# Seven zero matmuls ahead of the first projection, two staging tiles moved, and the last row block added up in PSUM

## The chip, the core and the metric

One core of a Trainium2 chip runs the whole program. The metric is the device time of one execution in microseconds (us): the kernel before takes 1064.06 us as the median of three runs (1063.52 to 1064.2). The core has five engines with a queue of instructions each: PE (matrix products; PEld is its loading of weights), DVE (vector), ACT (activations), POOL (general, slower) and SP, which here only issues transfers (DMA). A tile lies in SBUF or, for the sums that PE makes, in one of eight PSUM banks.

## The reference

A transformer block over 1024 tokens with 1024 features. Two groups of eight heads read one combined input projection; group A attends over a window of 128 tokens (two key/value heads, a sink per head), group B over nine chunks of 64 with a learned bias by distance.

```python
n = rms_norm(h, norm1_g[layer])
proj = jnp.einsum('bsd,dp->bsp', n, w_in[layer])
qa, ka, va, qb, kb, vb = jnp.split(proj, split_at, axis=-1)
ya = mixer_a(...); yb = mixer_b(...)
y = jnp.concatenate([rms_norm(ya, out_norm_a_g[layer]), rms_norm(yb, out_norm_b_g[layer])], axis=-1)
h = h + jnp.einsum('bsm,md->bsd', y, w_out[layer])
n2 = rms_norm(h, norm2_g[layer])
u = jnp.square(jax.nn.relu(jnp.einsum('bsd,df->bsf', n2, w_ff1[layer])))
h = h + jnp.einsum('bsf,fd->bsd', u, w_ff2[layer])
return rms_norm(h, final_norm_g)
```

All of it is float32. The kernel takes each product as three products of a high and a low part (high by high, high by low, low by high), summed in PSUM.

## The kernel before

**Start (L216 to L380).** The transposed input x comes in eight slices k of 128 features and two halves t of 512 tokens. `load_xT` (L225) loads a slice, ACT makes its high part (tile `nT`, L233), DVE the low part (L234). The weights of the first three projections, k, q and v of group A (`kA`, `qA0`, `vA`), are loaded and split the same way, those of kA and qA0 in four pieces between the slices. PE then runs, in an order that is written out and pinned from L342 on (`pe_order`): kA and qA0 by turns, two slices at a time, for t = 0 (48 matmuls of 128x512), vA for t = 0 (24), then kA, qA0 and vA for t = 1. After the third slice of kA, t = 1, four transposes turn the row scales `r` into a row `R` (`scales_along`).

`first_place` (L362) scales a projection by `R` into a staging tile `ts_...`, splits it into high and low (ACT L273, DVE or POOL L152) and sends it by 4 (q) or 8 (k) transfers into the tiles `QA` and `KA` that the scores read (L279, L282). For t = 0 the staging tile is one of the buffers that held x (`xs`); for t = 1 of k and q it is one of two buffers called `tst`, which `place` (L264) takes. The next projection, qA1, stages in `tst` too.

**Attention.** A planner interleaves units of attention with the remaining projections. A unit of group A makes scores (`S_A`), takes maxima on DVE (L438) and exponentials on ACT (L439), and normalises the probabilities `P_A`: DVE those of its first block, POOL those of its second (`POOL_NORM`, L545). PE transposes them (`pt_A`), ACT and DVE split the result (`T_A`, L446 and L152), PE multiplies by V (`av_A`). POOL's queue at that place holds, in this order: two scalings of a bias tile `b_A` (L470), the low parts of the weights of qA2 in four pieces (`w_qA`, L152), the two normalisations of the first unit, the low part of the staged qA1.

**SP's queue.** Transfers are issued in one order. Each of them reuses one of eight semaphores and so waits until the transfer eight places ahead has landed.

**Tail (L1198 to L1311).** The MLP's second product ends with the four row blocks 4 to 7 of the lower left quarter. `last_product` (L1276) adds 12 matmuls per block onto the bank that already holds the sum before; blocks 4, 6 and 5 are whole (512 columns), and DVE adds the bank to the residual `C` (tile `h`). For the last block, 7, DVE adds what the bank holds ahead of time (L1268), and the last product goes into two fresh banks `end0` and `end1` of 256 columns. `final` (L1198) is a generator per block: ACT squares and sums the rows, DVE and ACT make the reciprocal root `rf` of their mean, the rows are multiplied by it and the gain, and two transfers write the block out. In it, the halves (`fo`) of blocks 4, 5 and 6 are made by one DVE operation with the gains in PSUM (L1237) and by POOL and ACT (L1217, L1241). For block 7 DVE adds `end0` and `end1` to `C`, ACT squares `C`, POOL multiplies `C` by the gain (L1227), and at last DVE (640 columns) and ACT (384) multiply by `rf`. ACT issues the last transfer, SP the others (L1244).

## Time and profile before

| what | value |
|---|---|
| three runs, median (range) | 1064.06 us (1063.52 to 1064.2) |
| the profiled execution | 1064.61 us, of it 1062.5 us from its first to its last instruction (the span) |
| PE busy | 1048.2 us of the span |
| DVE, ACT, POOL busy | 702.4, 584.3, 421.1 us |
| first matmul, from the span's start | 5.04 us |

Times inside the span count from its start. A row of the timeline has start, duration, engine, line, operation, out<-in, shape and a count where like instructions are merged; square brackets tell how long the engine was idle before and what released it. PEclk is the share of TensorE's clock that was granted. The duration of a matmul goes from issue to its end, and matmuls overlap, so the pace of PE is read from the starts of groups.

### The profile page before, as it was taken

The numbers are of one execution on the slowest core, as the hardware profiler recorded it, in microseconds if no ns is written. First come the engines' busy times: TensorE is split into PE (matmuls) and PEld (weight loads), VectorE is DVE, ScalarE is ACT, GpSimd is POOL, SyncE is SP. The second block draws the span as 40 slices with busy tenths as digits, with TensorE's granted clock in tenths as the row PEclk, the third lists the DMA queues.
The fourth block names the chain that finished last, engine by engine and source line by source line (L and its number), as shares of the span: only waits on it lengthen the run. The fifth ranks groups of instructions, "written<-read, shape, count | busy, mean of one in ns | idle before, by whom it ended". The sixth has DMA issues, their size and how long they took to land.

```text
span 1062.5 us, 14416 instructions
## 1 busy us (share of the span) xinstructions
PE 1048.2 (99%) x5052; PEld 874.1 (82%) x5052; DVE 702.4 (66%) x1120; ACT 584.3 (55%) x1012; POOL 421.1 (40%) x326
## 2 busy tenths in 40 slices
PE   8999999999999999999999999999999999999997
PEld 6888888888888888888888888888888888888886
DVE  5577775767676765696534324436879877778667
ACT  7677786666574565675544554455533333333346
POOL 1476796334350243305564454345015024024026
PEclk9999999999999999999999999999999999999999
DMA  9954536253584442215544535416997535532004
GB/s 329 261 147 136 144 108 162 89 130 112 131 282 170 140 159 100 104 56 177 183 136 159 181 116 178 160 64 247 367 401 267 179 121 165 180 116 91 1 1 159
DMA packets 90440, 170.17 MB, mean 160 GB/s; under 512 B 7808, under 2 KB 43648, under 8 KB 90368
## 3 DMA queue, kind: packets, MB, share of 16 engines
q1 hardware_dynamic: 90080, 169.06, 48.1%
q8 instruction: 40, 0.66, 0.3%
q14 instruction: 32, 0.26, 0.1%
q10 hardware_dynamic: 288, 0.20, 0.1%
HBM read 105.26 MB, written 45.09 MB: 142 GB/s over the span
## 4 chain that ended last, share of the span: by engine, by line
PE 93%; DVE 3%; DMA 2%; ACT 1%; issue 1%; SPq 0%; DVEq 0%; ACTq 0%
PE f L146 27%; PE f_a L146 16%; PE f_c L146 8%; PE ip_qA L146 4%; PE op_B L146 4%; PE f_b L146 4%; PE ip_vB L146 4%; PE ip_qB L146 4%; PE op_A L146 4%; PE ip_kB L146 3%; PE av_B L146 3%; PE pt_B L149 2%; PE S_B L146 2%; PE S_A L146 1%; PE ip_kA L146 1%; PE av_A L146 1%
## 5 line engine op out<-in xcount | busy, mean ns | idle before, releaser
L146 PE MATMUL f<-X,W 128*128 128x512 f32 x1344 | 306.0, 389 | 0.1
L146 PEld LDWEIGHTS f<-X,W 128*128 128x128 f32 x1344 | 252.0, 188 | 52.9 <-DVE X L152 0.5
L146 PE MATMUL f_a<-V,U 128*128 128x512 f32 x756 | 173.6, 389 | 0.2 <-DVE bsf L137 0.2
L152 POOL TENSOR_TENSOR U<-u,U 128x1024 fp32r<-128x1024 f32 x32 | 80.4, 2512 | 226.9 <-PE f_c L146 134.9
L146 PEld LDWEIGHTS f_a<-V,U 128*128 128x128 f32 x756 | 141.9, 188 | 30.1 <-DVE bsf L137 0.6
L152 POOL TENSOR_TENSOR W<-T,W 128x1024 fp32r<-128x1024 f32 x29 | 75.6, 2609 | 141.6 <-ACT W L981 141.6
L146 PE MATMUL f_c<-V,U 128*128 128x512 f32 x384 | 88.4, 389 | 0.0
L146 PEld LDWEIGHTS f_c<-V,U 128*128 128x128 f32 x384 | 72.1, 188 | 15.0
L981 ACT ACTIVATE V<-Z 128x1024 fp32r<-128x1024 f32 x32 | 33.9, 1060 | 89.7 <-PE f_a L146 44.6
L1030 DVE TENSOR_TENSOR k<-f,k 128x1024 f32<-128x1024 f32 x24 | 29.3, 1221 | 60.7 <-PE f L146 60.7
L981 ACT ACTIVATE V<-w 128x1024 fp32r<-128x1024 f32 x24 | 25.4, 1060 | 78.9 <-issue 34.2
L152 POOL TENSOR_TENSOR W<-w,W 128x1024 fp32r<-128x1024 f32 x23 | 56.3, 2449 | 30.9 <-ACT W L981 30.8
L152 DVE TENSOR_TENSOR V<-w,V 128x1024 fp32r<-128x1024 f32 x24 | 47.6, 1985 | 27.1 <-ACT V L981 27.1
L981 ACT ACTIVATE U<-u 128x1024 fp32r<-128x1024 f32 x56 | 58.5, 1044 | 11.5 <-DMA ud<-k 7.1
L439 ACT ACTIVATE P_B<-P_B,nm_B 128x640 f32<-128x640 f32 (+2 forms) x64 | 44.3, 693 | 23.9 <-DVE nm_B L438 12.9
L1024 ACT ACTIVATE k<-f 128x1024 f32<-128x1024 f32 x24 | 24.6, 1026 | 59.1 <-PE f L146 59.1
L152 DVE TENSOR_TENSOR T_B<-pt_B,T_B 128x512 fp32r<-128x512 f32 (+2 forms) x72 | 39.7, 552 | 21.6 <-ACT T_B L446 21.3
L981 ACT ACTIVATE W<-T 128x1024 fp32r<-128x1024 f32 x32 | 33.9, 1058 | 35.5 <-PE f L146 21.1
L146 PE MATMUL ip_vB<-nT,w_vB 128*128 128x512 f32 x192 | 52.0, 399 | 0.9 <-DVE T_B L152 0.9
L146 PE MATMUL op_A<-w_o,y 128*128 128x512 f32 x192 | 52.2, 397 | 0.7 <-DVE h L773 0.4
L146 PE MATMUL ip_qB<-nT,w_qB 128*128 128x512 f32 x192 | 51.5, 396 | 0.0
L146 PE MATMUL ip_kB<-nT,w_kB 128*128 128x512 f32 x192 | 51.3, 396 | 0.0
(233 smaller groups left out, 2056.9 us busy)
## 6 DMA issues: line engine op xcount, KB each, us to landing
w<-in_w_ff_dram SPq DMA_DIRECT2D x64, 512.0 KB, 4.7
u<-ud SPq DMA_DIRECT2D x56, 512.0 KB, 4.7
ud<-k SPq DMA_DIRECT2D x48, 512.0 KB, 3.2
KkB<-ts_kB SPq DMA_DIRECT2D x64, 128.0 KB, 2.3
yd<-y SPq DMA_DIRECT2D x14, 512.0 KB, 2.8
y<-yd SPq DMA_DIRECT2D x14, 512.0 KB, 6.3
xs<-in_xT_dram SPq DMA_DIRECT2D x16, 256.0 KB, 5.3
xr<-in_x_dram SPq DMA_DIRECT2D x8, 512.0 KB, 7.0
```

Of the source, the lines that this page charges most:

```text
L146: pe(nc.tensor.matmul(*args, **kw))
L149: pe(nc.tensor.transpose(*args))
L152: engine.tensor_tensor(lo, full, f(hi), ALU.subtract)
L439: nc.scalar.activation(pr[:, :n], pr[:, :n], AF.Exp, bias=nm, scale=-1.0, accum_out=sm)
L981: nc.scalar.activation(w[0], full, AF.Copy)
L1024: nc.scalar.activation(kept[p], ps, AF.Copy)
L1030: dve.tensor_tensor(v, ps, v, ALU.add)
```

## The change

Three edits. First, a tile `busy` of 128x512 zeros is set by DVE, and PE multiplies it seven times into a PSUM tile that nobody reads, ahead of everything else; the tile takes one of the four buffers of `xr`, so that tile's pool is laid out in another order too. Second, `first_place` stages t = 1 of kA and qA0 in pages (a pool of 35 equal tiles) and no longer in `tst`. Third, for block 7 ACT copies the residual into the two banks `end0` and `end1`, the matmuls add onto it, and ACT squares and DVE multiplies by the gain straight from the banks; block 5's first half moves from DVE to two POOL operations.

```diff
@@ constants
+EARLY = 7
@@ start
     sps = sp_.enter_context(tc.tile_pool(name="sps", bufs=1, space=PSUM))
+    pe_order["on"] = True
+
+    busy = sp.tile([P, HALF], F32R, tag="xr", bufs=4, name="busy")
+    nc.vector.memset(f(busy), 0.0)
+    idle_ps = sps.tile([P, HALF], F32, tag="r", bufs=2, name="idle_ps")
+    for n in range(EARLY):
+        matmul(idle_ps, busy[:, :P], busy, start=n == 0, stop=n == EARLY - 1)
...
-    pe_order["on"] = True
     wk, k_steps = proj_weight(KA0, "kA", dve, 4)
...
-        st = sp.tile([P, 2, HALF], F32R, tag="xs", bufs=6, name=f"ts_{name}_{t}") if kind != "v" and t == 0 else None
+        st = None
+        if kind != "v":
+            st = page([P, 2, HALF], f"ts_{name}_{t}") if t else sp.tile([P, 2, HALF], F32R, tag="xs", bufs=6, name=f"ts_{name}_{t}")
@@ final
             ss, to = square(tmp[:, cs[0]], h[0], "last", base)
             base_of(ss, to, base)
+            if tb == 5:
+                pool.tensor_tensor(tmp[:, cs[0]], h[0], gfb[:, cs[0]], ALU.mult)
         else:
             for m in range(2):
                 c = slice(m * 2 * P, (m + 1) * 2 * P)
-                dve.tensor_tensor(h[0][:, c], ends[m], h[0][:, c], ALU.add)
-                ss, to = square(tmp[:, c], h[0][:, c], "last" if m else "0", base)
-                pool.tensor_tensor(tmp[:, c], h[0][:, c], gfb[:, c], ALU.mult)
+                ss, to = square(h[0][:, c], ends[m], "last" if m else "0", base)
+                dve.tensor_tensor(tmp[:, c], ends[m], gfb[:, c], ALU.mult)
...
-        if tb < 7:
+        if tb == 5:
+            pool.tensor_tensor(tmp[:, cs[0]], tmp[:, cs[0]], r.to_broadcast([P, HALF]), ALU.mult)
+        elif tb < 7:
             dve.scalar_tensor_tensor(tmp[:, cs[0]], h[0], r, gains[0][:, cs[0]], ALU.mult, ALU.mult)
@@ end
-    ends = [fps.tile([P, 2 * P], F32, tag=f"{'ab'[1 ^ g % 2]}1", bufs=1, name="end0")]
+    ends, rest = [], h
+
+    def end_bank(tag):
+
+        m = len(ends)
+        ends.append(fps.tile([P, 2 * P], F32, tag=tag, bufs=1, name=f"end{m}"))
+        in_order[1].activation(ends[m], rest[:, 2 * m * P : 2 * (m + 1) * P], AF.Copy)
+
+    end_bank(f"{'ab'[1 ^ g % 2]}1")
...
-                mm3(ps, ..., alone and n == n0 and i == 0, n > n0 and i == 1, True)
+                mm3(ps, ..., False, n > n0 and i == 1, True)
...
         before = finals[q]
         next(before)
-    last_product(ends[0], 3, slice(0, 2 * P), True)
+        if q == 2:
+            end_bank(f"{'ab'[g % 2]}1")
+    last_product(ends[0], 3, slice(0, 2 * P))
...
-    ends.append(fps.tile([P, 2 * P], F32, tag=f"{'ab'[g % 2]}0", bufs=1, name="end1"))
-    last_product(ends[1], 3, slice(2 * P, HALF), True)
+    last_product(ends[1], 3, slice(2 * P, HALF))
```

The changed kernel's lines are 1 to 21 higher than those before. On PE and DVE, at the very start, the order before is this, PE first (`nT_155` is a high part, `nT_159` a low part):

```order
L146 MATMUL ip_kA_324<-nT_155,w_kA 128x512
L146 MATMUL ip_kA_324<-nT_159,w_kA 128x512
L94 MEMSET ones 128x1
L96 MEMSET eps_76 128x1
L234 SCALAR_TENSOR_TENSOR nT_159<-xs_185,g1c,nT_155 128x512
```

And this with the change:

```order
L147 MATMUL idle_ps<-busy 128x512 x7
L147 MATMUL ip_kA_334<-nT_165,w_kA 128x512
L147 MATMUL ip_kA_334<-nT_169,w_kA 128x512
L95 MEMSET ones 128x1
L97 MEMSET eps_76 128x1
L223 MEMSET busy 128x512
L242 SCALAR_TENSOR_TENSOR nT_169<-xs_195,g1c,nT_165 128x512
```

Nothing else moves on these engines before the tail: one memset and seven matmuls are put in front.

On DVE, where qA1 is staged for the first time (`ts_qA_0`), the order with its waits is this before; the eight DMAHW are the semaphores of transfers:

```order
L438 ISA P_A_2_0_637,nm_A_2_633<-S_A_2_0_636,b_A_318,nsink 128x256 [waits PE_49]
L438 ISA nm_A_2_633 128x1
L152 TENSOR_TENSOR VA_176<-vt_vA_626,VA_176 128x8x64 [waits Activation_49]
L270 SCALAR_TENSOR_TENSOR ts_qA_0_654<-ip_qA_0_588,R_154 128x512 [waits DMAHW4_49,DMAHW3_49,DMAHW5_49,DMAHW2_49,DMAHW6_49,DMAHW1_49,DMAHW7_49,DMAHW0_49,PE_49]
L438 ISA P_A_2_1_667,nm_A_2_633<-S_A_2_1_666,b_A_318,nsink 128x256 [waits PE_49]
```

And this with the change:

```order
L447 ISA P_A_2_0_647,nm_A_2_643<-S_A_2_0_646,b_A_328,nsink 128x256 [waits PE_49]
L447 ISA nm_A_2_643 128x1
L153 TENSOR_TENSOR VA_186<-vt_vA_636,VA_186 128x8x64 [waits Activation_49]
L278 SCALAR_TENSOR_TENSOR ts_qA_0_664<-ip_qA_0_598,R_164 128x512 [waits PE_49]
L447 ISA P_A_2_1_677,nm_A_2_643<-S_A_2_1_676,b_A_328,nsink 128x256 [waits PE_49]
```

The order is the same; the wait for the transfers out of the staging tile is gone.

On DVE at the end of the program the order before is this (`fo_9430` is block 5, `fo_9450` block 7; `qf` and the second `wf` lead to the reciprocal root `rf`):

```order
L137 TENSOR_TENSOR C_7498<-end_9460,C_7498 128x256
L137 RECIPROCAL qf_9433<-uf_9431 128x1
L137 RECIPROCAL rf_9434<-wf_9432 128x1
L137 TENSOR_SCALAR bsf_0_9541<-ssf_0_9539,bsf_1_9457 128x1
L137 TENSOR_TENSOR C_7498<-end_9547,C_7498 128x256
L137 SCALAR_TENSOR_TENSOR fo_9430<-C_7496,rf_9434,gains 128x512
L137 TENSOR_SCALAR wf_9452<-ssf_last,bsf_0_9541 128x1
L137 RECIPROCAL qf_9453<-uf_9451 128x1
L137 RECIPROCAL rf_9454<-wf_9452 128x1
L137 TENSOR_SCALAR fo_9450<-fo_9450,rf_9454 128x640
```

And this with the change, with its waits (block 5 is `fo_9440` and its root `rf_9444`, block 7 `fo_9460`):

```order
L138 TENSOR_TENSOR fo_9460<-end_9470,gfb 128x256 [waits Activation_49]
L138 RECIPROCAL qf_9443<-uf_9441 128x1
L138 RECIPROCAL rf_9444<-wf_9442 128x1 [waits DVE_49]
L138 TENSOR_SCALAR bsf_0_9554<-ssf_0_9552,bsf_1_9467 128x1
L138 TENSOR_TENSOR fo_9460<-end_9513,gfb 128x256 [waits Activation_49]
L138 TENSOR_SCALAR wf_9462<-ssf_last,bsf_0_9554 128x1 [waits DVE_49]
L138 RECIPROCAL qf_9463<-uf_9461 128x1 [waits Activation_49]
L138 RECIPROCAL rf_9464<-wf_9462 128x1 [waits DVE_49]
L138 TENSOR_SCALAR fo_9460<-fo_9460,rf_9464 128x640 [waits DVE_49,Pool_49]
```

The two additions have become two products that wait for ACT's squares, and block 5's product has left DVE. POOL gains the two rows for it in place of its two products of 256 columns:

```order
L1226 TENSOR_TENSOR fo_9430<-C_7352,gfb 128x512
L1226 TENSOR_TENSOR fo_9440<-C_7352,gfb 128x512
L1226 TENSOR_TENSOR fo_9450<-C_7354,gfb 128x512
L1226 TENSOR_TENSOR fo_9460<-C_7354,gfb 128x512
L1232 TENSOR_TENSOR fo_9440<-C_7506,gfb 128x512
L1247 TENSOR_TENSOR fo_9440<-fo_9440,rf_9444 128x512
```

The last of these waits for DVE's `rf_9444`, and SP issues block 5's transfer from it ahead of block 7's.

More of the change, by code (lines that the diff above doesn't have):

```diff
@@ L1280, in last_product @@
             for i in range(2):
-                mm3(ps, (uh[:, i, c], ul[:, i, c]), (wh[:, i, cols], wl[:, i, cols]), alone and n == n0 and i == 0, n > n0 and i == 1, True)
+                mm3(ps, (uh[:, i, c], ul[:, i, c]), (wh[:, i, cols], wl[:, i, cols]), False, n > n0 and i == 1, True)
     for q in (0, 2, 1):
-        last_product(banks["a"][q // 2][:, q % 2], q, slice(0, HALF), False)
+        last_product(banks["a"][q // 2][:, q % 2], q, slice(0, HALF))
         h = acc[1, 0, q // 2][:, q % 2]
```

2 lines of the change are left out of this document (1 added, 1 removed).

## The prediction

> **What bounds the kernel now.** I read the page first, then the waits of PE, then the timeline of the first 60 us and of the last 10, since the change touches only those.
>
> ```profile
> PE 1048.2 (99%) x5052; PEld 874.1 (82%) x5052; DVE 702.4 (66%) x1120; ACT 584.3 (55%) x1012; POOL 421.1 (40%) x326
> PE 93%; DVE 3%; DMA 2%; ACT 1%; issue 1%; SPq 0%; DVEq 0%; ACTq 0%
> PE ip_kA L146 <- ACT w_kA L193: 5.0, 1, 5.0
> ```
>
> PE sets the time: 93% of the chain that ended last, and its one long wait is the 5.0 us before the first matmul. So the change can win only where PE is slow, waits, or has ended. It is slow at the start:
>
> ```profile
> 8.00:10.00 2.00, 2.00 (x6) 1.53 (x5) 1.83 (x4) 1.26 (x3) 0.00 (x0) 1.00 1.01 351
> L146 PE MATMUL ip_qA<-nT,w_qA x5: 628/628/628, 8.3 to 10.0; 128*128 128x512 f32 x5
> L146 PE MATMUL ip_qA<-nT,w_qA x16: 389/389/389, 13.1 to 19.3; 128*128 128x512 f32 x16
> 5.04 3.46 PE L146 MATMUL ip_kA<-nT,w_kA 128*128 128x512 f32 x6 [5.04 <-ACT w_kA L193]
> 8.31 2.76 PE L146 MATMUL ip_qA<-nT,w_qA 128*128 128x512 f32 x6
> 10.87 1.97 PE L146 MATMUL ip_kA<-nT,w_kA 128*128 128x512 f32 x6
> 12.67 1.53 PE L146 MATMUL ip_qA<-nT,w_qA 128*128 128x512 f32 x6
> 19.48 5.60 PE L146 MATMUL ip_vA<-nT,w_vA 128*128 128x512 f32 x24
> 24.92 2.20 PE L146 MATMUL ip_kA<-nT,w_kA 128*128 128x512 f32 x9
> 1056.00:1059.60 3.60, 0.24 (x3) 0.04 (x1) 2.60 (x9) 2.03 (x5) 1.45 (x2) 1.00 0.44 164
> 1059.70:1062.50 2.80, 0.00 (x0) 0.00 (x0) 0.00 (x0) 0.00 (x0) 0.00 (x0) 0.50 0.53 195
> ```
>
> The same matmul takes 628 ns up to 10 us and 389 ns from 13 us on. Six of them start in 10.87-8.31 = 2.56 us, 0.427 us each; later 24 start in 24.92-19.48 = 5.44 us, 0.227 each. The switch lies between 10.87 and 12.67, some 6.5 us after the first matmul. The clock column says 1.00 in the slow stretch too, so it is no witness there; but after PE's last work at 1056.24 it falls from 1.00 to 0.50 by 1059.7. PE's clock is halved when PE rests, and PE begins so. Trainium skill, "TensorE: Matmul & The Clock Gate", section "Part 1: The HAM clock gate (the "warmup" mystery)", has the same two paces, 426.7 and 215.7 ns, and the trace agrees on the first.
>
> **The zero matmuls.** What they cost, and what an earlier full clock is worth:
>
> ```profile
> 0.84 0.06 DVE L96 MEMSET eps<- 128x1 f32 x1
> 4.72 0.75 DVE L234 SCALAR_TENSOR_TENSOR nT<-xs,g1c,nT 128x512 fp32r<-128x512 f32 x1 [3.83 <-ACT nT L233]
> 7.29 0.50 PEld L146 LDWEIGHTS ip_kA<-nT,w_kA 128*128 128x128 f32 x2 [0.50 <-DVE nT L234]
> 13.95 0.75 DVE L234 SCALAR_TENSOR_TENSOR nT<-xs,g1c,nT 128x512 fp32r<-128x512 f32 x1
> 25.09 0.17 DVE L169 RECIPROCAL r<-w_n 128x4 f32<-128x4 f32 x1
> 26.96 0.60 PE L149 MATMUL r<-ident,r 128*128 128x128 f32 x4
> 30.83 5.60 PE L146 MATMUL ip_qA<-nT,w_qA 128*128 128x512 f32 x24
> ```
>
> No row has DVE's memset of 128x512. It follows the memset at 0.84 and lies between that row's 0.06 us and the 0.75 of DVE's 128x512 operation, so it ends between 1.0 and 1.65. Seven matmuls at 0.427 are 2.99 us: they end between 4.0 and 4.7, before the 5.04 at which the data is there, and DVE has nothing else before 4.72. They cost nothing; a start 0.4 later would begin to.
>
> If the clock is full by 7.29, the first projections run so: up to 7.29 PE waits for low parts of nT, as it does now, and from there 44 of the 48 k and q matmuls remain, 44 x 0.227 = 9.97, so vA starts at 17.26 and not at 19.48, 2.2 us earlier. The last low part is ready at 13.95+0.75 = 14.70 and PE wants it at 15.45; the others have more room. vA ends at 22.70. Then the first cut: the four transposes of r cannot start before 25.09+0.17, some 25.3, and from them to qA0, t = 1, it is 30.83-26.96 = 3.87 us. So qA0 starts at 29.2, and 1.65 of the 2.2 us is left.
>
> The second cut is where I expect most of the gain to go:
>
> ```profile
> SPq L282 <- DMA st_qA<-in_w_in_dram: 1.2, 1, 1.2
> 35.45 1.10 SPq L282 DMA_DIRECT2D KA<-ts_kA  x2
> 40.52 1.63 SPq L469 DMA_DIRECT2D b_A<-in_dist_dram  x2
> 45.69 1.77 POOL L470 TENSOR_SCALAR b_A<-b_A 128x256 f32<-128x256 f32 x2 [4.48 <-DMA b_A<-in_dist_dram]
> 47.52 2.82 POOL L152 TENSOR_TENSOR w_qA<-st_qA,w_qA 128x256 fp32r<-128x256 f32 x4
> 50.33 1.83 POOL L545 TENSOR_SCALAR P_A<-P_A,rc_A 128x256 f32<-128x256 f32 x2
> 53.01 0.37 PEld L149 LDWEIGHTS pt_A<-ident,P_A 128*128 128x128 f32 x2
> 51.81 0.69 DVE L270 SCALAR_TENSOR_TENSOR ts_qA<-ip_qA,R 128x512 f32<-128x512 f32 x1 [0.67 <-DMA QA<-ts_qA]
> 52.58 0.63 ACT L273 ACTIVATE ts_qA<-ts_qA 128x512 fp32r<-128x512 f32 x1 [1.13 <-DMA QA<-ts_qA]
> 55.24 0.84 ACT L446 ACTIVATE T_A<-pt_A 128x256 fp32r<-128x256 f32 x2
> ```
>
> The first two transposes of attention (pt_A) read probabilities that POOL normalises until 50.33+1.83 = 52.16. POOL gets to them by a chain that PE has no part in: it idles 4.48 us for the load of b_A, then scales it, splits four weight pieces, and normalises, with no gap from 45.69 to 52.16. And b_A lands when SP's order lets it: SP waits until 35.45 for the landing of st_qA, a load queued behind the input loads, and issues without a long pause from there to 40.52. None of this moves when PE is earlier. PE's second load for pt_A starts some 0.2 after 53.01; it can start at about 52.2. So PE keeps 1.0 us at most and stands still for the rest.
>
> **The staging pages.** They take away DVE's wait of 0.67 us and ACT's of 1.13 for the tiles to be sent. In the trace before PE loses nothing by these. They matter once PE is early: ACT reaches T_A at 55.24 only because its queue is late by them, and the matmul behind T_A would hold PE at today's time. Without them T_A comes some 0.7 us earlier, which is about the lead PE has. I take 0.9 us for the start as a whole; bounds are 0 (full clock no earlier) and 1.65 (POOL's chain earlier after all).
>
> **The tail.**
>
> ```profile
> 1053.21 3.03 PE L146 MATMUL end<-V,U 128*128 128x256 f32 x24
> 1056.28 0.42 DVE L137 TENSOR_TENSOR C<-end,C 128x256 f32<-128x256 f32 x1
> 1056.74 0.42 ACT L137 ACTIVATE fo<-C 128x256 f32<-128x256 f32 x1 [0.76 <-DVE C L137]
> 1057.06 0.19 ACT L137 ACTIVATION_READ_ACCUMULATOR fo<-C 128x1 f32 x1
> 1057.28 0.21 DVE L137 TENSOR_SCALAR wf<-ssf_last,bsf 128x1 f32<-128x1 f32 x1
> 1057.61 0.17 DVE L137 RECIPROCAL qf<-uf 128x1 f32<-128x1 f32 x1
> 1058.39 0.55 DVE L137 TENSOR_SCALAR fo<-fo,rf 128x640 f32<-128x640 f32 x1
> 1059.02 0.36 ACTq L1244 DMA_DIRECT2D out_dram<-fo  x1
> 1043.29 7.28 POOL L1217 TENSOR_TENSOR fo<-C,gfb 128x512 f32<-128x512 f32 x5
> ```
>
> PE ends at 1056.24. ACT's last square now starts there and not at 1056.74: 0.46 earlier, its sum read by 1056.79 instead of 1057.25. But DVE must do its product with the gain between that and wf, and waits for the square with it: 0.42 by the addition's row. So wf starts at about 1057.2, qf 0.2 later at 1057.4 instead of 1057.61, and the rest follows unchanged: 0.2 us gained, 0.3 if DVE's instructions overlap as in the rows, 0.46 if the product were hidden. On the other side is POOL: two products for block 5 at 7.28/5 = 1.46 us each. The first is done long before, the second starts after block 5's root, at some 1056.8, and ends at 1058.2; SP issues its transfer and then block 7's, which is ready at 1058.7. At 2.3 us instead of 1.46 it would delay SP past today's issue, so the lower bound is a loss of 0.3. ACT's two copies into the banks cost 0.42 each by the row of its 256 columns and lie in ACT's idle time. I take 0.25.
>
> **Sum.** 0.9 + 0.25 = 1.15: 1064.61 becomes 1063.46. This execution is 0.55 above the median of the three runs. Part of that may be the moment at which the clock became full, which the cap at POOL takes out of the new time, so I carry half of it: 1063.2, 0.08% under 1064.06.
>
> **Rivals.** First, the full clock does not come earlier. For: the stretch from 5.04 to 7.29, with gaps, did not bring it, and the one that did, from 7.29 to about 11.7, is 4.4 us without a gap; the zeros are 3 us, and a gap follows. Against: nothing that the trace can show. Only the tail is left: 1063.8. The same section of the skill's page says that activity is judged over free-running windows of 3413 ns; by that, 2.99 us never fill one, which speaks for this rival, and the phase would differ between executions.
>
> Second, PE keeps all 1.65 us, because POOL's chain is earlier too. For: the pool of the first tiles is laid out anew, so waits for buffers can shift. Against: the order of POOL and SP is the same and b_A waits for its load. It would be 1064.06-1.65-0.25 = 1062.15, and 1061.9 with the best tail.
>
> Third, the other side: the clock becomes full during the zeros, PE then has 5 matmuls in the 2.25 us up to 7.29, a load of half, and the clock falls back and must be earned again, later than today. The nearest row for a step of the clock is the 3.4 us from 1056.24 to 1059.7; one more such step at half pace is 8 matmuls x 0.2 = 1.6 us, and lateness meets no cover: 1064.06+1.6-0.25 = 1065.4. It decides if 628 ns comes back after the first 389.
>
> **Chances.** Forecast 0.55 (1063.2, within about 0.6), clock no earlier 0.25, all of 1.65 kept 0.13, clock falling back 0.07. The range 1061.9 to 1064.3 takes in the first three and leaves out the last and what is beyond the bounds. A difference of 0.2% is 2.13 us, about what can be told from no change here. Faster than that, under 1061.93, needs the second rival with the best tail, or a gain that I have not seen: 0.13. Slower, over 1066.19, needs the third with more than one step: 0.03. The rest, 0.84, is within.
>
> **What would show it.** Right: matmuls of 389 ns before 8 us, vA near 17.3, qA0 (t = 1) near 29.2, then PE idle for up to 0.7 us before pt_A with POOL as the releaser, pt_A near 52.2, no DMA wait at ts_qA, and the last output issued 0.2 to 0.3 us sooner after PE's end. Wrong: 628 ns up to 11 us; pt_A at 51.4; POOL still at work on block 5 after 1058.6; or PE waiting anywhere after 60 us where it does not now.

## The result, and the profile after

| kernel | median of 22 runs | range | its profiled execution | span |
|---|---|---|---|---|
| before | 1064.16 us | 1063.02 to 1065.05 | 1064.61 us | 1062.5 us |
| changed | 1066.18 us | 1064.74 to 1067.47 | 1064.74 us | 1062.6 us |

The ratio is 1.0019 [1.0014, 1.0025]: the change makes the kernel 2.0 us slower, where 0.9 us faster was forecast. The profiled execution of the changed kernel is the fastest of its 22, so its trace shows less of the loss than the median has; a second run of the same kernel (`again`, below) gave 1065.85 us, and its trace agrees with the first one in every point made here.

The start came as computed. Rows of the changed kernel's page (busy time; shares of the chain that ended last), of the matmuls into `ip_qA` in its first 12 us (shortest, median and longest in ns, first and last start), and its PE timeline:

```profile
PE 1050.3 (99%) x5059; PEld 874.1 (82%) x5059; DVE 700.6 (66%) x1120; ACT 585.2 (55%) x1014; POOL 424.5 (40%) x326
PE 89%; DVE 4%; DMA 2%; ACT 2%; issue 1%; POOL 1%; SPq 0%; DVEq 0%; ACTq 0%; POOLq 0%
```

```profile
L147 PE MATMUL ip_qA<-nT,w_qA x12: 388/391/398, 7.1 to 11.6; 128*128 128x512 f32 x12
```

```profile
1.51 3.35 PE L147 MATMUL idle_ps<-busy 128*128 128x512 f32 x7 [1.51 <-DVE busy L223]
4.94 2.27 PE L147 MATMUL ip_kA<-nT,w_kA 128*128 128x512 f32 x6
...
17.23 5.60 PE L147 MATMUL ip_vA<-nT,w_vA 128*128 128x512 f32 x24
...
25.27 0.65 PE L150 MATMUL r<-ident,r 128*128 128x128 f32 x4
...
51.59 0.38 PE L150 MATMUL pt_A<-ident,P_A 128*128 128x128 f32 x2
```

The zeros end at 4.86, just ahead of the first real product. No matmul of `ip_qA` takes 628 ns any more; the slowest takes 398. vA starts at 17.23 (before 19.48), the transposes of `r` at 25.27, qA0 for t = 1 at 29.19, 1.64 us earlier than before.

The cut that POOL was to make did not come. POOL's timeline after:

```profile
44.58 1.77 POOL L479 TENSOR_SCALAR b_A<-b_A 128x256 f32<-128x256 f32 x2 [4.44 <-issue]
...
49.23 1.83 POOL L554 TENSOR_SCALAR P_A<-P_A,rc_A 128x256 f32<-128x256 f32 x2
```

It has normalised at 51.06 and not at 52.16, and PE starts `pt_A` at 51.59 (the last row of PE above), still 1.64 us ahead of before.

So PE comes out of the start with the whole lead. It then loses it, and this is where: waits of PE between 15 us and its end, the changed kernel first, then the kernel before (us in total, times, longest).

```profile
PE pt_B L150 <- DVE T_B L153: 1.3, 2, 1.1
PE ip_vB L147 <- DVE T_B L153: 0.9, 1, 0.9
...
PE av_B L147 <- DVE padL L153: 0.2, 1, 0.2
```

```profile
PE ip_vB L146 <- DVE T_B L152: 0.9, 1, 0.9
...
PE pt_B L149 <- DVE T_B L152: 0.3, 2, 0.2
PE op_A L146 <- DMA y<-yd: 0.2, 1, 0.2
```

The 0.9 us of `ip_vB` is in both. New is one wait of 1.1 us before `pt_B`, far from everything that the change touches. Here are both kernels' DVE, POOL and PE rows around it (attention's group B, some 260 us after the last edited line of the start), before first. DVE's `y` is the low part of an output `Y` of attention times its gain. `sqB` is POOL's running sum of the squares of `Y`; the `y` that its row reads is another tile, `y2` in the code, so neither of the two operations reads the other's result. `T_B` is the split of transposed probabilities for which PE waits:

```profile
312.35 0.29 DVE L152 TENSOR_TENSOR padF<-pt_B,padF 128x128 fp32r<-128x128 f32 x1 [0.50 <-ACT padF L446]
312.63 0.69 DVE L267 TENSOR_TENSOR ts_vB<-ip_vB,R 128x512 f32<-128x512 f32 x1
...
314.30 0.75 DVE L678 SCALAR_TENSOR_TENSOR y<-Y,ogc,y 128x512 fp32r<-128x512 f32 x1
314.58 1.61 POOL L501 TENSOR_TENSOR sqB<-sqB,y 128x512 f32<-128x512 f32 x1
...
315.57 0.66 PE L149 MATMUL pt_B<-ident,P_B 128*128 128x128 f32 x4 [0.15 <-DVE T_B L152]
```

```profile
311.40 0.29 DVE L153 TENSOR_TENSOR padF<-pt_B,padF 128x128 fp32r<-128x128 f32 x1 [0.33 <-ACT padF L455]
312.05 0.69 DVE L275 TENSOR_TENSOR ts_vB<-ip_vB,R 128x512 f32<-128x512 f32 x1 [0.35 <-PE S_B L147]
...
313.63 1.30 POOL L510 TENSOR_TENSOR sqB<-sqB,y 128x512 f32<-128x512 f32 x1
313.73 1.74 DVE L687 SCALAR_TENSOR_TENSOR y<-Y,ogc,y 128x512 fp32r<-128x512 f32 x1
...
315.99 0.66 PE L150 MATMUL pt_B<-ident,P_B 128*128 128x128 f32 x4 [1.15 <-DVE T_B L153]
```

Two things are to be seen. First, before, DVE goes from `padF` to `ts_vB` without a pause; after, it stands still for 0.35 us there. The row names PE's `S_B`, but `ts_vB` reads nothing of it, and before it started while `S_B` was still running: nothing that the trace shows holds it. Second, that 0.35 turns an order round. Before, DVE starts `y` 0.28 ahead of POOL's `sqB`: 0.75 us for DVE, 1.61 for POOL. After, POOL is first by 0.10: 1.30 us for POOL, and DVE's operation of the same shape takes 1.74. Whoever comes second seems to stand still until the first is done, and when that is DVE, `T_B` comes 1 us late and PE waits. The Trainium skill, "SBUF — State Buffer", section "Who interferes with whom", has it that DVE and GpSimd (POOL here) share a pair of SBUF ports, that a DVE instruction with two SBUF inputs contends for it with a GpSimd instruction that reads SBUF, and that whoever issues first takes the pair as an exclusive lock; 0.75 against 1.74 us and 1.61 against 1.30 agree with that.

At the end (ACT, POOL and DVE of the changed kernel, then how long its last transfers took from issue to landing, last column, then the same of before):

```profile
1056.23 0.38 ACT L138 ACTIVATE C<-end 128x256 f32<-128x256 f32 x1 [0.73 <-PE end L147]
...
1056.68 1.04 POOL L1247 TENSOR_TENSOR fo<-fo,rf 128x512 f32<-128x512 f32 x1 [0.50 <-DVE bsf L138]
...
1057.96 0.56 DVE L138 TENSOR_SCALAR fo<-fo,rf 128x640 f32<-128x640 f32 x1
1058.60 0.35 ACTq L1256 DMA_DIRECT2D out_dram<-fo  x1
```

```profile
out_dram<-fo SPq DMA_DIRECT2D x1, 320.0 KB, 3.2
out_dram<-fo ACTq DMA_DIRECT2D x1, 192.0 KB, 2.8
```

```profile
out_dram<-fo SPq DMA_DIRECT2D x1, 320.0 KB, 2.5
out_dram<-fo ACTq DMA_DIRECT2D x1, 192.0 KB, 2.7
```

The last output is issued 0.4 us sooner (1058.60 against 1059.02; 2.68 us after PE's last matmul start against 3.06), as meant. But SP's 320 KB now take 3.2 us to land and not 2.5, so the sooner issue is worth nothing: from PE's last matmul start to the last landing it is 5.70 to 5.74 us in all ten traced executions with the old end, 5.85 to 5.87 with the new one (once 6.06).

How PE stands against the kernel before (start of the same matmul minus its start before, us; negative is earlier; median over the 10 us from each time) sums this up, with kernels of the experiments:

| kernel | 40 | 60 | 290 | 330 | 1050 |
|---|---|---|---|---|---|
| changed | -1.64 | -1.64 | -1.59 | -0.03 | -0.05 |
| `again` (the same) | -1.27 | -1.27 | -1.30 | +0.08 | +0.10 |
| `zeros` | -1.38 | +0.22 | +0.22 | +1.11 | +1.09 |
| `pages` | -1.15 | -1.15 | -0.93 | +0.83 | +0.86 |
| `tail` | -1.04 | -1.02 | -1.04 | -1.51 | -1.54 |
| `pad` | -0.10 | -0.06 | -0.01 | -0.49 | -0.38 |
| `pool_after` | -1.60 | +0.55 | +0.62 | +0.49 | +0.48 |
| `tiny_alone` | -1.35 | +0.33 | +0.37 | +0.56 | +0.59 |
| `before_loads_later` | -1.37 | -1.33 | -1.31 | -1.76 | -1.76 |
| `mended_old_end` | -1.60 | -1.05 | -0.84 | -0.70 | -0.76 |

In these kernels two stages move it, 48 to 56 us and 295 to 320 us; nothing else between 40 and 1050 does by more than 0.3 us. And the column at 40 holds a surprise: `pages`, `tail`, `tiny_alone` and `before_loads_later`, without a single full-sized zero matmul, are also 1.0 to 1.4 us ahead there. The profiled execution of before is simply late.

### The profile page after: what moved, and what is told of

It is laid out like the page before. It is cut to its first block, busy times and chain, and to the rows that moved or that the text cites. A ratio compares the mean times of both kernels' runs of the same rounds, so it can differ in the third digit from the quotient of the medians.

```text
span 1062.6 us, 14420 instructions
## 1 busy us (share of the span) xinstructions
PE 1050.3 (99%) x5059; PEld 874.1 (82%) x5059; DVE 700.6 (66%) x1120; ACT 585.2 (55%) x1014; POOL 424.5 (40%) x326
## 4 chain that ended last, share of the span: by engine, by line
PE 89%; DVE 4%; DMA 2%; ACT 2%; issue 1%; POOL 1%; SPq 0%; DVEq 0%; ACTq 0%; POOLq 0%
PE f L147 27%; PE f_a L147 16%; PE f_c L147 8%; PE op_B L147 4%; PE f_b L147 4%; PE ip_qB L147 4%; PE op_A L147 4%; PE ip_qA L147 4%; PE ip_kB L147 3%; PE ip_vB L147 3%; PE av_B L147 3%; PE pt_B L150 2%; PE S_B L147 2%; PE S_A L147 1%; PE av_A L147 1%
## 5 line engine op out<-in xcount | busy, mean ns | idle before, releaser
L153 DVE TENSOR_TENSOR V<-w,V 128x1024 fp32r<-128x1024 f32 x24 | 47.7, 1990 | 27.0 <-ACT V L990 27.0
L455 ACT ACTIVATE T_B<-pt_B 128x512 fp32r<-128x512 f32 (+2 forms) x72 | 34.9, 485 | 30.4 <-PE pt_B L150 30.1
```

The lines of the kernel that those rows point to most:

```text
L153: engine.tensor_tensor(lo, full, f(hi), ALU.subtract)
L455: nc.scalar.activation(T[:, 0, lo:hi], tp, AF.Copy)
```

## The experiments

Each kernel was timed together with the kernel before on the same chip, and "over before" means over that median: 1063.77 us for `zeros`, `pages`, `tail` and `again`; 1063.84 for `pad`, `pool_after`, `dve_more` and `tiny`; 1063.81 for `tiny_alone`, `loads_later`, `mended` and `mended_old_end`; 1063.94 for `before_loads_later`, `tiny_loads_later`, `old_end_less` and `new_end_less`; 1063.81 for `later_again` and `split_first`. Three letters recur in the expectations: P is the pause of DVE with the turned order at 312 us, F the fetching of PE's instructions, which added entries shift, D a bound by transfers at the end. A matmul and its weight load are two entries in PE's queue.

### Each edit alone, and the whole again

`zeros` has the first edit only, `pages` the second, `tail` the third.

```diff
# zeros
+    pe_order["on"] = True
...
+    for n in range(EARLY):
+        matmul(idle_ps, busy[:, :P], busy, start=n == 0, stop=n == EARLY - 1)
# pages
+            st = page([P, 2, HALF], f"ts_{name}_{t}") if t else sp.tile([P, 2, HALF], F32R, tag="xs", ...)
# tail
...
-                dve.tensor_tensor(h[0][:, c], ends[m], h[0][:, c], ALU.add)
...
+                ss, to = square(h[0][:, c], ends[m], "last" if m else "0", base)
+                dve.tensor_tensor(tmp[:, c], ends[m], gfb[:, c], ALU.mult)
...
```

> The kernel before with the seven zero matmuls alone. The changed kernel's median is 2.0 us over the kernel before (1066.18 against 1064.16), while its one profiled execution, the fastest of all, shows PE 1.6 us ahead until 300 us and level from 320 us on. Theory A, the start disturbs a later stage: the lead of 1.6 us is lost in the stage at 300 to 320 us, where PE waits for transfers of y, and in most executions more than the lead is lost there; then this kernel is 1.5 to 2.0 us over the kernel before, and PE in its profile is 1.6 us ahead at 290 us. Theory B, the tail costs the 2 us: this kernel is within 0.4 us of the kernel before, the lead being used up by 320 us. Theory C, the lead needs the staging pages: without them PE waits behind T_A near 55 us and is less than 1.0 us ahead at 60 us.

> The kernel before with the two staging pages alone. All theories: within 0.3 us of the kernel before, and no wait for a transfer at ts_qA near 52 us. A median more than 1 us over the kernel before would say that the place of the two tiles in the memory, or the buffers of pages that become free later, is what costs the 2 us.

> The kernel before with the new end alone. The prediction's step: 0.25 us under the kernel before (0.46 under to 0.3 over). From the profile of the changed kernel: the last output is issued 0.4 us sooner after PE's end, but block 5's and block 7's transfers, 1 MB, are now issued within 0.93 us instead of 1.63 and the last lands 0.1 us later in the span, so 0.0 to 0.2 over. Theory B, the tail costs most of the 2 us: 1.0 to 2.0 us over the kernel before.

> The changed kernel once more, for a second profile and beside the three single edits on the same chip. Its time less that of the kernel before should be 1.5 to 2.5 us (2.0 in the first comparison). If its profiled execution is one of the ordinary, slower ones, the stage that loses the time shows in it: theory A expects PE 1.6 us ahead at 290 us and 1 to 2 us behind at 330 us, and level from there to the end; theory B expects it level at 1050 us and behind at the end.

| kernel | median (range) | ratio to before |
|---|---|---|
| `zeros` | 1066.09 (1065.1 to 1067.87) | 1.0021 [1.0012, 1.0031] |
| `pages` | 1064.70 (1064.22 to 1065.38) | 1.0007 [0.9999, 1.0016] |
| `tail` | 1064.08 (1063.32 to 1064.92) | 1.0003 [0.9994, 1.0012] |
| `again` | 1065.85 (1064.36 to 1066.83) | 1.0019 [1.0011, 1.0028] |

The zeros alone are slower by 2.3 us, as much as the whole change; each of the other two is at most a little slower, and no single edit is faster. The three losses (2.3, 0.9, 0.3) come to more than 2.0. Two reasons show in the traces: `zeros` and `pages` both lose at the pause of 312 us, which the whole change pays only once, and `zeros` also loses at 52 to 56 us what the pages save. The trace of `zeros` also shows what the staging pages are good for (DVE, then PE):

```profile
52.37 0.69 DVE L278 SCALAR_TENSOR_TENSOR ts_qA<-ip_qA,R 128x512 f32<-128x512 f32 x1 [2.25 <-DMA QA<-ts_qA]
...
56.21 0.85 PE L147 MATMUL av_A<-T_A,VA 128*128 128x256 f32 x2 [0.84 <-ACT T_A L453]
```

Without them DVE waits 2.25 us for the staging tile to be sent, ACT's `T_A` is late behind it, and PE loses all of its lead there (-1.38 to +0.22).

### The pause of DVE and the lock with POOL

`pad` adds four one-column memsets to DVE's queue at the start, so that later instructions take other places in it. `pool_after` makes POOL's `sqB` of that place wait for DVE's `y`; for that it writes the split of `Y` and the transfer of it ahead of the sum in the program. `dve_more` is the kernel before, with DVE doing half of that `ts_vB` twice, which puts in about the time of the pause. `tiny` is the changed kernel with zero matmuls of 2 columns: the same entries, but hardly any work that could warm the clock.

```diff
# pad
     nc.vector.memset(f(busy), 0.0)
+    for _ in range(4):
+        nc.vector.memset(eps4, EPS / 4)
# pool_after, for m = 6, t = 0
...
+                    split_y(y, Y, self.m)
+                    nc.sync.dma_start(yd[self.m, :, t], f(y))
+                    add = nc.gpsimd.tensor_tensor(acc, acc, y2, ALU.add)
+                    tc.add_manual_dep(add.ins, last_low[0], dep, reason="after the low part of y")
...
# dve_more, on the kernel before, for vB3, t = 1
+                nc.vector.tensor_tensor(f(st[:, 0, : 2 * P]), acc[:, : 2 * P], R1[:, h], ALU.mult)
# tiny
-        matmul(idle_ps, busy[:, :P], busy, start=n == 0, stop=n == EARLY - 1)
+        matmul(idle_ps[:, :2], busy[:, :P], busy[:, :2], start=n == 0, stop=n == EARLY - 1)
```

> The changed kernel with four memsets of 128x1 more at DVE's start, where DVE waits for data anyway (4 x 0.03 us). In the profiles of the changed kernel (twice), of the zeros alone and of the pages alone, DVE halts some 0.4 us with nothing to wait for at the same place of its queue, the 704th recorded entry: there that is ts_vB at 312 us, in the kernel before and the tail alone it is padF, four entries earlier, where DVE idles for ACT anyway. Behind the halt DVE's low part of y (128x512) comes 0.1 us after POOL's sum sqB instead of 0.28 us before it, and takes 1.74 to 1.77 us instead of 0.75; PE then waits 1.2 us for T_B at pt_B instead of 0.2. Theory P, the halt belongs to the place in the queue and tips the order of DVE and POOL: with four entries more it falls on padF again; y takes 0.75, the wait at pt_B is 0.2, and the time is 1.0 to 1.4 us under the changed kernel, 0.6 to 1.0 over the kernel before. Theory L, the lead of PE itself makes DVE late there: no change, 1.8 to 2.2 us over the kernel before.

> The changed kernel with one wait more: POOL's sum sqB of this pair of heads starts after DVE's low part of y, so that the two cannot overlap. Theory P: the halt of 0.4 us at ts_vB stays, y takes 0.75 us, PE's wait at pt_B falls from 1.2 to 0.2-0.3, and the time is 1.0 us under the changed kernel, about 1.0 over the kernel before. Theory L, or if the long y is not made by POOL: y stays near 1.75 us and the time does not change.

> The kernel before with the suspected delay put in by hand: DVE does the first 256 of the 512 columns of this one ts_vB twice, some 0.35 us more on DVE ahead of T_B and y. Theory P: y then starts behind POOL's sqB, takes 1.7 us, PE waits 1.2 us at pt_B, and the time is 1.0 to 1.4 us over the kernel before, three to four times what was put in. Theory L: 0 to 0.4 us over it.

> The changed kernel with its seven zero matmuls on 2 columns instead of 512: as many instructions on every engine, but PE is not kept busy and the clock is earned where it was before, between 8.2 and 11.7 us. Theory P: the halt at ts_vB and the long y are there, and the time stays 1.0 us or more over the kernel before; PE's lead over the profiled execution of before at 290 us is between 0 and 1.2. Theory L: without the early clock the loss goes; 0 to 0.9 over the kernel before, no more than the pages alone.

| kernel | median (range) | ratio to before |
|---|---|---|
| `pad` | 1065.25 (1064.07 to 1066.66) | 1.0015 [1.0006, 1.0024] |
| `pool_after` | 1065.25 (1063.51 to 1066.27) | 1.0010 [1.0001, 1.0018] |
| `dve_more` | 1065.46 (1064.63 to 1066.4) | 1.0016 [1.0007, 1.0025] |
| `tiny` | 1065.90 (1064.56 to 1067.38) | 1.0018 [1.0010, 1.0027] |

DVE and POOL at the place, of `pad`, of `pool_after` and of `dve_more`:

```profile
312.32 0.29 DVE L153 TENSOR_TENSOR padF<-pt_B,padF 128x128 fp32r<-128x128 f32 x1 [0.77 <-ACT padF L457]
312.59 0.69 DVE L277 TENSOR_TENSOR ts_vB<-ip_vB,R 128x512 f32<-128x512 f32 x1
...
314.27 0.75 DVE L689 SCALAR_TENSOR_TENSOR y<-Y,ogc,y 128x512 fp32r<-128x512 f32 x1
314.55 1.61 POOL L512 TENSOR_TENSOR sqB<-sqB,y 128x512 f32<-128x512 f32 x1
```

```profile
315.25 0.75 DVE L696 SCALAR_TENSOR_TENSOR y<-Y,ogc,y 128x512 fp32r<-128x512 f32 x1
...
316.14 1.28 POOL L515 TENSOR_TENSOR sqB<-sqB,y 128x512 f32<-128x512 f32 x1 [1.04 <-DVE y L696]
```

```profile
313.41 0.42 DVE L269 TENSOR_TENSOR ts_vB<-ip_vB,R 128x256 f32<-128x256 f32 x1
...
315.36 1.29 POOL L504 TENSOR_TENSOR sqB<-sqB,y 128x512 f32<-128x512 f32 x1
315.55 1.65 DVE L681 SCALAR_TENSOR_TENSOR y<-Y,ogc,y 128x512 fp32r<-128x512 f32 x1
```

With DVE's queue shifted, the pause is gone from `ts_vB`, DVE is first again, and `y` takes 0.75. With POOL held back it takes 0.75 too. With nothing but 0.42 us of DVE work put into the kernel before, POOL is first, `y` takes 1.65, PE loses 1.84 us between 290 and 330 (1.1 of it before `pt_B`), and the median is 1.6 us higher. So P is shown from both sides: the order of two instructions that miss each other by 0.1 to 0.3 us is worth a microsecond to PE. In the medians `pad` and `pool_after` each took back 0.64 us of 2.05 (1.41 remains over before). The size of that is uncertain, since their intervals overlap the changed kernel's, 1.0014 to 1.0025. `tiny` says what the loss is not: there the clock is not early (matmuls of 628 ns up to 10 us), PE has no more lead than other kernels, and the loss is 2.06 us all the same; `y` takes 1.77 us.

The pause itself follows a place in DVE's queue: it sits at the 704th recorded entry, `ts_vB` or the wait ahead of it, in `zeros`, `pages`, `tiny`, `pool_after`, `again` and the changed kernel (0.33 to 0.35 us). In before, `tail` and `pad` that place is `padF`, where DVE waits for ACT in any case and the pause costs nothing. The count is not exact: in `loads_later`, `mended`, `mended_old_end` and `split_first` the 704th entry comes just after `padF` or `ts_vB`, and no pause shows there. What halts the engine no record tells.

`pool_after` also shows the other stage, unasked (PE, and the transfers into `QA` between 48 and 55.5 us with their median time to landing):

```profile
55.03 0.71 PE L148 MATMUL S_A<-KA,QA 128*128 128x256 f32 x4 [1.54 <-DMA QA<-ts_qA]
```

```profile
QA<-ts_qA SPq DMA_DIRECT2D x4, 128.0 KB, 5.3
```

It differs from the changed kernel by one edit at 312 us, and yet this execution lost the whole lead at 55 us, to transfers that took 3.7 us there (the three of them issued in this window) and 5.3 here.

### Entries in PE's queue, and the transfers at 50 us

At 48 to 56 us the transfers of K and Q for t = 1 run beside loads of weights that are not needed soon. `tiny_alone` is before with seven float32 matmuls of 2 columns ahead; each goes out as two, so there are 28 more entries (the zeros of the change are 14). The four `loads_later` kernels issue the weights of qA3 and kB behind K's and Q's transfers: on the changed kernel, on before (twice), and on `tiny_alone`. `split_first` is `mended_old_end` (below) with 12 of the first real matmuls cut in two, 24 entries more; the first sums of kA and qA0 lose a product in half of their columns by it, which changes those sums.

```diff
# tiny_alone, on the kernel before
...
+    for n in range(7):
+        matmul(idle_ps[:, :2], ident, ident[:, :2], start=n == 0, stop=n == 6)
# loads_later, before_loads_later, tiny_loads_later, later_again
+        if name == "qA3":
+            last_load[0] = q_sent
...
-    first_place(1, 1, accs[1])
+    q_sent = first_place(1, 1, accs[1])
# split_first
...
+                for a, b in ((w[0], n[0]), (w[0], n[1]), (w[1], n[0])):
+                    for h in (slice(0, 2 * P), slice(2 * P, HALF)):
+                        matmul(acc[:, h], a[:, k], b[:, h], ...)
```

> The kernel before with seven matmuls of 2 columns at PE's start and nothing else: no early clock, no other queue changed, only PE's instructions stand 14 places later. Theory F: the fetch of PE's instructions moves from 54.9 us into the transfers of QA, t = 1, at about 51 to 53 us, QA lands up to 1.5 us later, and since PE without a lead wants it only at 54.9, the median rises by 0.0 to 0.8 us. Theory P has no say here: DVE's queue is as before, y takes 0.75 us. More than 0.8 over the kernel before would mean that the place of PE's fetches costs time elsewhere too.

> The changed kernel with the loads of two weights (of qA3 and of kB) issued behind the transfers of K and Q, t = 1, instead of ahead of them. Why: in the profile of the kernel in which POOL was made to wait, PE was 1.6 us ahead until 52 us and then waited 1.5 us in S_A for QA<-ts_qA, which landed at 55.42; in ten profiles it lands between 52.67 and 55.42, and in all six with seven more matmuls a fetch of PE's instructions (16 KB, 1.2 us on one DMA engine) falls into these transfers, at 48.7 to 50.7 us, where the kernels without them have it near 54.9. Theory F, in most executions the changed kernel loses 1 us or more there, which its profile did not show: QA now lands before 52.0, S_A does not wait, and the median is 0.7 to 1.3 us under the changed kernel (0.8 to 1.4 over the kernel before, the loss at 313 us remains). Without theory F: within 0.3 of the changed kernel.

> The kernel before with the two loads later and nothing else. Its K and Q are there in time in every profile, so theory F expects no more than 0.3 us either way. A gain of 0.5 us or more would say that the kernel before loses time there too in its ordinary executions, and would be a version that beats both.

> The kernel before with the seven tiny matmuls, which alone cost 1.4 us (1065.19 against 1063.81), and the two loads later. Theory F, the fetch of PE's instructions costs by falling into the transfers of K and Q, t = 1: with room ahead of PE the loss goes, and the median is within 0.4 of the kernel with later loads alone. If the 1.4 us come from the place of PE's fetches elsewhere, they stay.

> The kernel before with the two loads later, a second time: 0.2 to 0.8 us under the kernel before (first time 1063.41 against 1063.94).

> The kernel with all three mendings and the old end, with the first 12 real matmuls (kA and qA0, two slices) split into two of 256 columns each: the same sums, 24 more entries in PE's queue (12 matmuls, 12 weight loads), in the stretch where PE waits for data. Theory F, the place of the fetches counts: yd is written with no fetch of PE's within it, lands about 3 us after its issue instead of 4.57, PE keeps its lead over 300 to 320 us (shift there -0.4 to -0.5 as in the kernels without more entries, instead of +0.1), and the median is 0.4 to 0.8 us under the unsplit kernel's 1063.67, that is 0.5 to 1.0 under the kernel before. If yd lands in 3 us and the time stays, the write of yd does not set the stage; if yd still takes 4.5 us, the fetch was not moved far enough and nothing is learned.

| kernel | median (range) | ratio to before |
|---|---|---|
| `tiny_alone` | 1065.19 (1064.12 to 1065.83) | 1.0013 [1.0004, 1.0022] |
| `loads_later` | 1064.18 (1063.47 to 1065.11) | 1.0005 [0.9996, 1.0014] |
| `before_loads_later` | 1063.41 (1062.78 to 1064.24) | 0.9996 [0.9987, 1.0005] |
| `tiny_loads_later` | 1064.63 (1063.74 to 1066.4) | 1.0005 [0.9996, 1.0014] |
| `later_again` | 1063.43 (1062.67 to 1064.47) | 0.9998 [0.9989, 1.0007] |
| `split_first` | 1063.56 (1063.12 to 1069.05) | 0.9999 [0.9990, 1.0008] |

Nothing but some microscopic matmuls before the first real one makes the kernel 1.4 us slower. Its trace shows the same place as that of `zeros` (DVE, PE):

```profile
52.47 0.69 DVE L274 SCALAR_TENSOR_TENSOR ts_qA<-ip_qA,R 128x512 f32<-128x512 f32 x1 [1.49 <-DMA QA<-ts_qA]
...
56.31 0.84 PE L146 MATMUL av_A<-T_A,VA 128*128 128x256 f32 x2 [0.66 <-ACT T_A L449]
```

The DMA engines that carry the data also fetch instructions, in blocks. The profile page of the changed kernel has a queue of such blocks:

```profile
q8 instruction: 40, 0.66, 0.3%
```

These are forty fetches of 16 KB (0.66 MB in all), each of 0.9 to 1.9 us on one DMA engine. PE has 10,118 matmuls and weight loads, so there is one for some 250 of them, and the fetches move when PE alone gets more entries; so I take them for PE's. In the traces without added entries one of them starts at 52.6 to 57.1 us; with added entries it starts at 47.7 to 50.7, among the transfers of K and Q.

The other place is at 296 to 303 us, where a 512 KB piece (`yd`) is written to memory. SP's next transfer reads it back and waits for it, 2.4 us in the changed kernel and 0.8 before. A load of weights stands behind that one in SP's queue, and ACT waits for these weights (4.15 us, before 3.34), then DVE and at last PE. Issue to landing of the piece, in the changed kernel, in before and in `tail`:

```profile
yd<-y SPq DMA_DIRECT2D x1, 512.0 KB, 4.6
```

```profile
yd<-y SPq DMA_DIRECT2D x1, 512.0 KB, 3.0
```

```profile
yd<-y SPq DMA_DIRECT2D x1, 512.0 KB, 2.9
```

It took 2.6 to 3.0 us in kernels without added entries and 3.3 to 4.6 with them. A fetch starts during or just after the write in all of them, so its place alone does not tell them apart. The packets do. The write is 128 packets of 4 KB, and its landing is reported in 16 parts (us):

| kernel | the fetch | start of the last packets | 15th part | 16th part |
|---|---|---|---|---|
| before | 299.62 to 300.98 | 299.40, 299.55 | 299.92 | 300.30 |
| `before_loads_later` | 298.24 to 299.58 | 298.09, 298.24 | 298.62 | 298.85 |
| changed | 298.31 to 299.28 | 298.14, 299.26 | 298.33 | 300.32 |
| `loads_later` | 298.49 to 299.43 | 298.44, then 299.41, 299.84, 300.12 | 298.97 | 300.88 |

In before the last packet has started when the fetch begins. In the changed kernel 15 parts are there at 298.33, but the last packet starts only as the fetch ends, and the last part lands 2.0 us after the others. The first packet that is held up starts within 0.02 us of the end of the fetch in six traces: the changed kernel, `again`, `tiny`, `loads_later`, `mended` and `mended_old_end`. The records do not tell which DMA engine a packet is on, but six such coincidences leave little doubt that the fetch and this part of the write share one and that the write waits there. It is not all: in `zeros`, `pad` and `pool_after` (3.3 us) the fetch begins after the last packet has started. At 50 us the same sign is weaker. The last part of a transfer of Q is at most 0.5 us behind the 15th in the traces without added entries. In those with them the largest lag is 0.55 to 1.5 us, but only 0.3 in the first trace of the changed kernel, which is its fastest execution.

What this costs in time is less certain. `tiny_alone` lost more than F expected (0 to 0.8), and `tiny_loads_later` got back 0.69 of its 1.38 us over before where F expected all: the rest stays at 55 us (`T_A`) and at 309 to 313 (`padL`). `old_end_less` (below), without one added entry, lost 1.7 us at the first place in its trace, so added entries make the loss likelier and are not the only way to it. In `split_first` the fetch begins 0.1 us after the issue of the write, which lands in 3.6 us in place of `mended_old_end`'s 4.6, and PE gains 0.45 us over the 300 us stage, as F expected. But its median is that of the kernel without the split within the noise, so it does not settle what the loss is worth; its profiled execution lost 5.4 us elsewhere, at 820 us, where the granted clock was halved for 3.41 us, which no other trace has.

With the loads out of the way Q lands at 50.5 to 51.7 us in place of 52.7 to 55.4 (`tiny_loads_later`: 53.2). That is worth 1.7 us to the changed kernel (2.05 to 0.37 over before; by accident its DVE also missed the turned order at 312, so both places are in this number) and 0.5 and 0.4 us to the kernel before. That last one is the fastest kernel of all, though each interval by itself holds 1. Beside it the change still costs 0.8 us by the medians, with the same later loads in both (`loads_later` 0.37 over before, the other two 0.53 and 0.38 under).

### The end

Both ends without the transfer of block 5's first half, 256 KB that then do not reach the output: `old_end_less` with the old end, `new_end_less` with that of `tail`.

```diff
         for j in range(2):
+            if (tb, j) == (5, 0):
+                continue
             queue = nc.scalar if j and tb == 7 else nc.sync
```

> The kernel before without the transfer of block 5's first half to the output (256 KB, left out; everything else is computed). By theory D, the output in flight sets the end, 256 KB less at some 390 GB/s are up to 0.65 us; but here the transfers are 0.6 to 0.8 us apart and the last lands 2.5 to 2.7 us after its issue: 0.0 to 0.4 us under the kernel before.

> The same transfer left out of the kernel with the new end alone. Theory D: here the four last transfers are issued within 0.93 us and queue up, so without one of them the last lands 0.4 to 0.65 us sooner, 2.5 us after its issue instead of 3.2, and the gain that the prediction saw comes out: 0.2 to 0.4 us under the old end without the same transfer. Against it, a last transfer that lands 3.2 us after its issue as before, and a median no lower than the old end's.

`old_end_less` 1064.09 (1063.2 to 1065.84), ratio 1.0000 [0.9991, 1.0008]; `new_end_less` 1063.73 (1062.58 to 1065.03), 0.9999 [0.9990, 1.0008]. The two medians are 0.36 us apart, the way that D expected, but within the noise. The traces are clearer: from PE's last start to the last landing the old end takes 5.71 us, as with the transfer; the new end takes 5.33, down from 5.87. The last 320 KB (`new_end_less`):

```profile
out_dram<-fo SPq DMA_DIRECT2D x1, 320.0 KB, 2.4
```

It is 2.4 us again and not 3.2. So D holds: the new end wins its 0.4 us of computing, and loses it, and 0.15 more, because POOL makes block 5's half later than DVE did (its transfer is issued 1.76 us after PE's last start, before 1.42), so that the last 1 MB is sent within 0.93 us in place of 1.64 and the last piece queues.

### The mendings together

`mended` is the changed kernel with `pad`, `pool_after` and the later loads; `mended_old_end` the same with the end of before.

```diff
# mended_old_end against mended
...
-                ss, to = square(h[0][:, c], ends[m], "last" if m else "0", base)
-                dve.tensor_tensor(tmp[:, c], ends[m], gfb[:, c], ALU.mult)
+                dve.tensor_tensor(h[0][:, c], ends[m], h[0][:, c], ALU.add)
+                ss, to = square(tmp[:, c], h[0][:, c], "last" if m else "0", base)
+                pool.tensor_tensor(tmp[:, c], h[0][:, c], gfb[:, c], ALU.mult)
...
```

> The changed kernel with all three mendings: two loads later, four memsets more at DVE's start, POOL's sum behind DVE's low part of y. Theories P and F together say that nothing else costs time: PE's lead of 1.3 to 1.6 us over the profile of before (0.6 to 0.9 over its typical execution) lives through 53 and 313 us to the end; median 0.5 to 1.0 us under the kernel before. If it stays over the kernel before, a third place costs time that no profile has shown yet.

> As the kernel with all three mendings, but with the end of the kernel before (edits one and two alone). The prediction's step says 0.25 us slower than with the new end; the single edit (1064.08 against 1063.77) and the profile after say 0.0 to 0.3 faster, because the new end's last 1 MB of output is issued within 0.93 us instead of 1.63 and has to go out at the rate of the DMA engines anyway.

`mended` 1064.31 (1063.63 to 1064.86), ratio 1.0004 [0.9995, 1.0013]; `mended_old_end` 1063.67 (1062.65 to 1064.63), 1.0000 [0.9991, 1.0009]. By the medians the mendings take back 1.5 of the 2.0 us and the old end 0.64 more; that last step is not clear of the noise. `mended_old_end` is 0.14 us under before, which cannot be told from zero. It also holds the later loads, which alone bring before 0.4 to 0.5 us. So what is left of the change, an early clock and staging pages, has no gain to show even here. Its trace still loses 0.55 us at 55 us and its `yd` takes 4.6 us.

## Why the prediction was wrong

**The zero matmuls and the first cut: right.** At the start they cost nothing (what their entries cost later is told below), vA starts at 17.23 (17.26 said), the transposes of `r` at 25.27 (25.3), qA0 at 29.19 (29.2). The first rival, no earlier clock, fell: the zeros took 3.35 us and not 2.99, and the real products follow 0.08 us behind them, so the 3.4 us up to 5.91, where the clock became full, were filled by both together. Nor did the clock fall back, the third rival.

**What that is worth: the term was mis-sized.** "1.65 of the 2.2 us" was measured against one execution, and that one was late. Without zeros the clock became full at 8.2 to 12.6 us, and in the profiled execution of before at 11.74, nearly the latest. At 40 us the eleven traced executions without full-sized zeros (itself among them) are on the mean 0.74 us ahead of it, the nine with full-sized zeros 1.26: the edit is worth about 0.5 us there, not the 1.65 that were worked out nor the 0.9 that the sum took. In the medians not even that shows: `tiny`, with the same entries and no early clock, is 2.06 us over before, the changed kernel 2.05. The prediction saw that its execution was 0.55 above the median and suspected the clock, and carried half of it; it should have asked how far the switch can move, since the switch was the very thing that the edit changes.

**The second cut by POOL: wrong, and it hid nothing.** "None of this moves when PE is earlier" failed. SP's queue did move: K's transfers follow PE's products, they were issued from 29.14 (before 29.78), `b_A`'s load went out at 39.29 (before 40.52), and POOL was done 1.1 us sooner. So the second rival was right at this place, as the prediction's own sign ("pt_A at 51.4") would have it, though the reason is SP's queue and not the new layout of the tiles that it gave; its forecast of the time was still 4 us off, because of what came later.

**The staging pages: right.** Without them (`zeros`) the lead is lost at 52 to 56 us through `ts_qA` and `T_A`, as worked out.

**The tail: the chain was right, the end of it wrong.** The last output is issued 0.42 us sooner, 0.38 counted from PE's last start (0.2 to 0.3 said), POOL is done with block 5 at 1057.72, before 1058.6. But the sum stopped at the issue and took for granted that the rest "follows unchanged". The transfers are the rest: 0.25 gained became 0.15 lost from PE's end in the traces, 0.3 (`tail` against before) to 0.64 (`mended` against `mended_old_end`) by medians, neither of them clear of the noise.

**The step that was missing** is the largest. The prediction argued that "the change touches only" the first 60 us and the last 10, and carried the lead to the end unchanged: no term and no rival for the 990 us between. "They cost nothing" was said of the work of the zeros; that they also put 14 entries into PE's queue stands in no term. The order of instructions is the same there, but their places in the queues and their times against the other engines and the DMA are not. The sign named at the end, "PE waiting anywhere after 60 us where it does not now", is what happened: 1.1 us at 315.99. The sum that the runs support: the pause and the lock 0.65 us (`pad`, `pool_after`) to 1 (the wait in the trace); added entries with the transfers at 50 and 300 us, 1 to 1.4 us (`tiny_alone`, which has 28 entries more and not 14, 1.4); the new end 0.15 to 0.6; less 0.5 for the clock. That gives 1.3 to 2.5 us or so against 2.0 measured. In the second term, that a fetch holds up the write at 300 us is read from the packets; how much of the term it makes stays open.

## What to carry to other kernels

A gain at the start of a program that is bound by one engine has to survive every later place where two other engines miss each other by a few tenths of a microsecond; look for such places (a DVE operation with two SBUF inputs next to a POOL operation, transfers that land just in time) before carrying a lead through. An edit that only adds entries to a queue is not free even if its work is hidden: try it with entries that do no work. Time an end by the last landing and not by the last issue, and do not size a gain against one execution in the very thing that varies between executions.

## What the runs showed of the hardware

- **The switch to full clock varies by more than an edit is worth.** Without zeros it came 8.2 to 12.6 us after the span's start for the same first matmuls, with zeros 4.4 to 7.7, and once 11.1 (`pad`). The stretches of full clock are whole numbers of one period: 1047.89, 1054.72 and 1051.31 us are 307, 309 and 308 times 3.4133. The Trainium skill, "TensorE: Matmul & The Clock Gate", section "Part 1: The HAM clock gate (the "warmup" mystery)", gives free-running windows of 3413 ns, and these lengths agree; its spread of ±500 ns for the switch is too small for these runs.
- **DVE halts at one place in its queue** for 0.33 to 0.35 us with nothing to wait for, the 704th recorded entry in six traces, though four others show no pause at that count. Four memsets at the start moved it to an instruction that waits anyway, and the median fell by 0.64 us.
- **The lock between DVE and POOL** costs DVE 1.0 us on an operation of 0.75 us when POOL is first, POOL 0.3 when DVE is.
- **Entries without work** cost 1.4 us in a kernel of 1064 (`tiny_alone`). Its trace loses 1.65 us at 55 us and 0.2 at 310, both behind transfers that land just in time.
- **A fetch of instructions holds up a transfer.** A fetch of 16 KB takes about 1 us of one DMA engine. In six traces a packet of a 512 KB write started within 0.02 us of the end of such a fetch, and the last of its 16 parts landed 1.8 to 2.0 us after the 15th, against 0.0 to 0.4 in traces without added entries.
